# Attention outputs joined on ScalarE and GpSimd instead of VectorE, and one swap in the order of the up product

## The chip, the cores and the metric

The kernel runs on one core of a Trainium2 chip. The metric is the device time of one execution in microseconds (us). A core has five engines that each work through a list of instructions in order: TensorE (PE; its weight loads are shown apart, as PEld), VectorE (DVE), ScalarE (ACT), GpSimd (POOL) and SyncE (SP), which here only issues DMAs. Engines wait for each other by semaphores. Matmul results land in PSUM, in banks of 512 float32 columns on 128 partitions; everything else is in SBUF.

## The reference

One transformer block on 1024 tokens of width 1024, all in float32. Two mixers run on the same normalised input: softmax attention with a forget gate (8 heads of 64), and an RWKV-7 recurrence. Their outputs are gated, merged and projected; a feed-forward part with a short convolution and a gate follows.

```python
u = modulate(rms_norm(h, ln1_g), shift1, scale1)
proj = u @ w_in                                   # q, k, v, f | rwkv | gates
logits = q @ k.T * scale + cum[:, None] - cum[None, :]
o_fox = softmax(where(causal, logits, -inf)) @ v  # per head, 64 wide
merged = sigmoid(p_gate_fox) * (o_fox @ fox_w_out) + sigmoid(p_gate_rwkv) * (o_rwkv @ rwkv_w_out)
h = h + gate1 * (merged @ w_o)
u2 = modulate(rms_norm(h, ln2_g), shift2, scale2)
a, b = split(u2 @ w_up)                           # 2816 columns each
h = h + gate2 * ((silu(conv3(a) + conv_b) * b) @ w_down)
return rms_norm(h, final_g)
```

## The kernel before

Every float32 matrix is held as two parts of the fast matmul type, a high part (a rounded copy, made on ScalarE or GpSimd) and a low part (the rest, by a VectorE subtraction); a product is then three matmuls, high by high, high by low and low by high. Stages follow each other: the input projection, the RWKV recurrence, attention, the branch projections (br), w_o, the up product, and the down product.

**Attention.** Query rows are taken 256 at a time, so each head has four groups I, and a group goes through these steps:

- lg: the logits of two row blocks go to a PSUM bank pair. `softmax` takes the row maximum on VectorE (L1049, into nm), the exponential with its sum on ScalarE (L1053, into P), the reciprocal and the scaling of P on VectorE (L1058, L1059).
- tp: TensorE transposes P. `halve` copies the high part to th on ScalarE (L1086) and makes the low part tl on VectorE (L1089).
- ov: TensorE multiplies the values vh, whose 128 columns hold the high and the low part of 64 value columns, by th and tl. The result fills one bank of 128 rows by 256 columns: 64 rows of the high part's product and 64 of the low part's. There is one such bank, ov_ps.
- `collect` adds the two halves of the bank's rows: ScalarE copies one half to o (L1120), VectorE adds the other half from PSUM (L1122). When both heads of a pair have filled o, GpSimd splits it into fx (L1129, L1130); in the last head ScalarE and VectorE do that.

Between these steps TensorE computes the gate products (rk_ps, one bank) that were left over from before. ScalarE and VectorE evacuate them (`gate_out`, L1162 to L1170). GpSimd also casts their weights (hi_in, L266) and issues the loads of the next heads (stA L995, stB L997, vh L999), each of which waits until the tile it overwrites has been read.

The order of all this on TensorE, VectorE and ScalarE is written by a planner, class Weave, while the program is built. It holds a clock for TensorE, by the cost of each matmul, and clocks for ScalarE and VectorE, which `weave.use` moves by a cost; every chain yields the time until its next step is due, and gate products fill TensorE's time in between. `ov_free` holds the planned time at which the bank is free. GpSimd's and SyncE's instructions in this stage are placed by the framework's scheduler.

After attention, `br_load` loads a branch weight (raw_br, L1210) and `br_open` casts it, the first on GpSimd (L1223), the others on ScalarE (L1221), and loads a gate (L1226). The first br products are br0 and br1 of the first token half.

**Up product.** It is computed as a seven-product scheme per pair of column tiles: (i, k) is product k for tile i, with one operand made from w_up (A or S, high part on ScalarE L1481, low part on VectorE L1485) and one made from the activations (B11, T3, T2, T4, T1, B22; `T_split`, ScalarE L1722, VectorE L1724). Product 4 uses T4, product 5 uses T1, product 3 uses B22. Products 1, 6, 5 and 3 of one i add up in one bank, X; 7 and 4 in another, Y. Between them `up_evac` reads the sum so far: L1559 copies, L1564 adds Y into U after product 4, L1566 adds X into Z after product 5 (for i = 0 and 1 that tile is called Ze). The table `plan` sets the order of products; `up_to` makes the operands a few products ahead, and here SP, VectorE, ScalarE, GpSimd and TensorE all run in the order of the code. For i = 0 and 1 the T matrices themselves are still being made between the first products.

Of the kernel before, what the change touches and what calls it, by code (L numbers as in the profile page):

```python
# [9 lines left out]
F32 = mybir.dt.float32  # L10
F32R = mybir.dt.float32r
AF = mybir.ActivationFunctionType
ALU = mybir.AluOpType
# [119 lines left out]
def hybrid_block(ctx: ExitStack, tc: tile.TileContext, a, out):  # L133
    nc = tc.nc
    weave = Weave()
# [30 lines left out]
    def V(name, i=0, n=1):  # L166
        o, _ = VEC[name]
        return vec[:, o + i : o + i + n]
# [12 lines left out]

    omu = cp.tile([128, 14], F32, name="omu")
    nc.vector.tensor_scalar(omu, V("mu", 0, 14), -1.0, 1.0, op0=ALU.mult, op1=ALU.add)
    nw0 = cp.tile([128, 4], F32, name="nw0")
    nc.vector.tensor_scalar(nw0, V("w0", 0, 4), -1.0, None, op0=ALU.mult)
    na0 = cp.tile([128, 4], F32, name="na0")
    nc.vector.tensor_scalar(na0, V("a0", 0, 4), -1.0, None, op0=ALU.mult)
    nkk = cp.tile([128, 4], F32, name="nkk")
    nc.vector.tensor_scalar(nkk, V("k_k", 0, 4), -1.0, None, op0=ALU.mult)
    oka = cp.tile([128, 4], F32, name="oka")  # L190
    nc.vector.tensor_scalar(oka, V("k_a", 0, 4), -1.0, 1.0, op0=ALU.mult, op1=ALU.add)
    sc = cp.tile([128, 8], F32, name="sc")
    sig_c = nc.scalar.activation(sc, V("c", 0, 8), AF.Sigmoid)
# [794 lines left out]
    at = es.enter_context(tc.tile_pool(name="at", bufs=2, reuse_waits="tile"))  # L988
# [21 lines left out]
    with tc.manual_schedule(engines={mybir.EngineType.DVE, mybir.EngineType.Activation}):  # L1010
        seq = [(h, I) for h in range(8) for I in ((0, 1, 3, 2) if h == 7 else (3, 0, 2, 1))]
        lg_free, tp_free, pl_free, ps_free, th_free, ov_free = (deque([0.0] * n) for n in (2, 2, 4, 2, 3, 1))
        probs, av_queue, halves = {}, deque(), {}
        ov_ps = pb.tile([128, NH], F32, tag="big", name="ov")[:, 0:256]
        rk_ps = pb.tile([128, NH], F32, tag="big", name="rk_ps")

# [28 lines left out]
                    yield 0  # L1045

        def softmax(h, i, n, lg):
            nm = at.tile([128, 3], F32, tag="nm", name=f"nm{h}_{i}", bufs=4)
            nc.vector.tensor_reduce(nm[:, 0:1], lg[:, 0:n], axis=AX.X, op=ALU.max, negate=True)  # L1049
            yield weave.use("DVE", weave.now, 70 + 1.04 * n) + 140 - weave.now  # L1050
            e = (at.tile([128, S], F32, tag="P", name=f"P{h}_{i}", bufs=4) if i > 3 else
                 at.tile([128, NH], F32, tag="Ps", name=f"P{h}_{i}", bufs=2))
            nc.scalar.activation(e[:, 0:n], lg[:, 0:n], AF.Exp, bias=nm[:, 0:1], accum_out=nm[:, 1:2])  # L1053
            t = weave.use("ACT", weave.now, 250 + 0.83 * n)
            if i > 3 or i % 2:
                lg_free.append(t + 210)
            yield t + 140 - weave.now
            nc.vector.reciprocal(nm[:, 2:3], nm[:, 1:2])  # L1058
            ts(e[:, 0:n], e[:, 0:n], nm[:, 2:3], None, op0=ALU.mult)  # L1059
            t = weave.use("DVE", weave.now, 230 + 0.53 * n)  # L1060
            probs[h, i] = t + 210, e
# [32 lines left out]
        def a_chain():  # L1094

            for _ in range(8 * 10):
                while not av_queue:
                    yield 100
                t, h, I, jj, th, tl = av_queue.popleft()
                yield t - weave.now  # L1100
                if jj == 0:
                    yield from slot(ov_free)
                vh = heads[h][2]
                order = [(0, th), (1, th), (1, tl), (0, tl)] if jj == I else [(0, th), (0, tl), (1, th), (1, tl)]
                for x, (k, t) in enumerate(order):
                    o0 = 128 if (jj == I and k == 1) else 0
                    mm(ov_ps[:, o0:256], vh[:, 2 * jj + k, :], t[:, 256 * k : 256 * k + 256 - o0],
                       start=jj == 0 and x == 0, stop=jj == I and x == 3)
                th_free.append(weave.now + 260)
                if jj == I:  # L1110
                    weave.spawn(collect(h, I), 260)
                yield 0

        def collect(h, I):
            p, hf, oc = h // 2, I // 2, slice(I % 2 * 256, I % 2 * 256 + 256)
            rows = slice(h % 2 * 64, h % 2 * 64 + 64)
            if (p, hf) not in halves:
                halves[p, hf] = at.tile([128, NH], F32, tag="o", name=f"o{p}{hf}"), []
            o, got = halves[p, hf]
            nc.scalar.copy(o[rows, oc], ov_ps[rows, :])  # L1120
            yield weave.use("ACT", weave.now, 270) + 140 - weave.now
            tt(o[rows, oc], o[rows, oc], ov_ps[64 - h % 2 * 64 : 128 - h % 2 * 64, :], op=ALU.add)  # L1122
            t = weave.use("DVE", weave.now, 340) + 140
            ov_free.append(t + 70)
            got.append(I)
            if len(got) == 4:
                cs = slice(hf * NH, hf * NH + NH)
                if h < 7:
                    nc.gpsimd.tensor_copy(fx[0][p][:, cs], o)  # L1129
                    nc.gpsimd.tensor_tensor(fx[1][p][:, cs], o, f32(fx[0][p][:, cs]), op=ALU.subtract)  # L1130
                    return
                yield t - weave.now
                nc.scalar.copy(fx[0][p][:, cs], o)
                yield weave.use("ACT", weave.now, 530) + 140 - weave.now
                tt(fx[1][p][:, cs], o, f32(fx[0][p][:, cs]), op=ALU.subtract)
# [95 lines left out]
    if "rest" in marks:  # L1231
        g, m = (gsp.tile([128, NH], F32, tag="sp0", name=f"rest{k}") for k in range(2))
        i = nc.scalar.activation(g, marks["rest"], AF.Abs)
# [89 lines left out]
    for x in range(2):  # L1323
        for n in range(8):
            if x or n:
                k = 8 * x + n + 1
# [277 lines left out]
        put(6, s1[:, NH:])  # L1604

    plan = [(i, k) for ks in ((1, 2), (7,), (6,)) for i in range(2) for k in ks]
    plan += [(0, 4), (0, 5), (1, 5), (1, 4), (0, 3), (1, 3)] + [(2, k) for k in (1, 7, 6, 2, 4, 5)]
    for i in range(3, NFF):
        plan += [(i, 1), (i, 7), (i - 1, 3)] + [(i, k) for k in ((6, 2, 4, 5) if i < NFF - 1 else (6, 2, 5, 4))]
    plan.append((NFF - 1, 3))  # L1610
# [116 lines left out]
    for n in range(4):  # L1727
# [4 lines left out]
        if n in (1, 2):  # L1732
            kts = (0, 1) if n == 1 else (2, 3)
            turn2(1, [kt + 4 * j for kt in kts for j in range(2)], (2, 3, 4, 5), [U[j][kt] for kt in kts for j in range(2)],
                  rows=((0, 1, 2), (3,)) if n == 1 else ((0, 1, 2, 3),), by_dve=(1, 3) if n == 2 else ())
# [302 lines left out]
```

## Time and profile before

| what | value |
| --- | --- |
| median of three timed runs | 1654.52 us |
| the three runs | 1647.03, 1654.52, 1655.5 us |
| profiled execution, its own time | 1648.91 us |
| its span, first to last instruction | 1647.1 us |
| granted TensorE clock | 0.995 of full speed |
| attention outputs (first to last ov product) | 640 to 820 us |
| T4 and T1 made, first products with them | 1025 to 1043 us |

The profile is one execution. Its views name instructions by line, engine, operation and tiles (out<-in). A row of a timeline gives start, length, the instruction, and in brackets the idle time of the engine before it and what ended it. A row of waits gives who waited, for whom, total us, how often, and the longest. A row of groups gives busy us, the mean of one in ns, and the idle time before.

### The profile page before, as it was taken

The page shows a single profiled execution, that of the slowest core. Times are in us where ns is not written, and L with a number is a line of the kernel's source. Part 1 is how long each engine was busy: PE and PEld are TensorE (multiplying, and loading weights), DVE is VectorE, ACT ScalarE, POOL GpSimd, SP SyncE. Part 2 cuts the span into 40 slices and gives each one's busy share as a digit, 9 for nine tenths or more (in the row PEclk, how much of TensorE's full clock was granted, in tenths as well). Part 3 has the DMA queues.
Part 4 walks back from the last instruction along what each step waited for, and adds up shares of the span by engine and source line. Part 5 has one row for each costly group of instructions (what it writes and reads, how often), then busy time and mean ns, then how long its engine had stood idle before and what let it go on. Part 6 is the DMA issues. An engine that isn't in the chain of part 4 may idle for free.

```text
span 1647.1 us, 25947 instructions
## 1 busy us (share of the span) xinstructions
PE 1607.8 (98%) x9694; PEld 1339.6 (81%) x9694; DVE 1222.6 (74%) x2373; ACT 820.9 (50%) x1537; POOL 130.8 (8%) x153
## 2 busy tenths in 40 slices
PE   7999999999999999999999999999999999999998
PEld 7777788798978788888888888788888888888886
DVE  5786787878876526888679447887777777886677
ACT  5563335445445646766623235644444444555455
POOL 0011101111111010221022000000000000000000
PEclk9999999999999999999999999999999999999999
DMA  8488645543332346433197420242232232675363
GB/s 339 138 326 242 178 123 143 134 123 94 107 115 85 97 126 157 129 117 106 56 353 270 168 81 26 84 134 97 96 119 98 96 109 96 225 254 160 122 211 109
DMA packets 121645, 240.59 MB, mean 146 GB/s; under 512 B 40048, under 2 KB 48880, under 8 KB 121520
## 3 DMA queue, kind: packets, MB, share of 16 engines
q1 hardware_dynamic: 113040, 220.58, 41.0%
q0 software_dynamic: 8480, 18.37, 4.2%
q8 instruction: 76, 1.25, 0.3%
q14 instruction: 49, 0.40, 0.1%
HBM read 173.35 MB, written 65.54 MB: 145 GB/s over the span
## 4 chain that ended last, share of the span: by engine, by line
PE 58%; DVE 5%; ACT 2%; DMA 2%; issue 1%; SPq 0%; ACTq 0%; DVEq 0%
PE X L141 13%; PE D L141 13%; PE Y L141 6%; PE wo L141 5%; PE br L141 4%; PE rk_ps L141 3%; PE W L141 3%; PE gt L141 3%; PE lg L141 2%; PE ov L141 2%; PE tp L145 2%; DMA d_gate<-gs 1%; DVE nm L1049 1%; DVE P L1059 1%; DVE tl L1089 0%
## 5 line engine op out<-in xcount | busy, mean ns | idle before, releaser
L141 PE MATMUL D<-op,op 128*128 128x512 f32 x924 | 209.8, 389 | 0.0
L141 PEld LDWEIGHTS D<-op,op 128*128 128x128 f32 x924 | 173.3, 188 | 36.3 <-DVE op L1261 0.3
L141 PE MATMUL X<-T_m,S 128*128 128x512 f32 x440 | 107.8, 390 | 1.6 <-ACT T_m L1722 1.1
L141 PEld LDWEIGHTS X<-T_m,S 128*128 128x128 f32 x440 | 82.4, 188 | 20.4 <-ACT T_m L1722 2.5
L1260 ACT CAST op<-g 128x512 fp32r<-128x512 f32 x77 | 47.8, 621 | 73.8 <-PE D L141 49.0
L1261 DVE TENSOR_TENSOR op<-g,op 128x512 fp32r<-128x512 f32 x77 | 53.0, 688 | 41.4 <-ACT op L1260 41.4
L1519 DVE SCALAR_TENSOR_TENSOR c<-ab,vec,c 128x512 f32<-128x512 f32 x88 | 65.9, 750 | 18.4 <-ACT c L1522 16.8
L784 DVE TENSOR_TENSOR t<-E,M 128x60 f32<-128x60 f32 (+24 forms) x248 | 55.6, 224 | 27.9 <-DMA M<-sm 21.8
L1485 DVE TENSOR_TENSOR A<-ur,A 128x512 fp32r<-128x512 f32 x64 | 44.0, 688 | 38.7 <-ACT A L1481 38.5
L1485 DVE TENSOR_TENSOR S<-ur,S 128x512 fp32r<-128x512 f32 x66 | 45.5, 691 | 35.2 <-ACT S L1481 35.1
L274 DVE TENSOR_TENSOR lo_in<-raw_in,hi_in 128x512 fp32r<-128x512 f32 x84 | 56.7, 712 | 17.6 <-PE gt L141 4.8
L1481 ACT CAST S<-ur 128x512 fp32r<-128x512 f32 x66 | 41.0, 622 | 55.8 <-DVE ur L1474 30.6
L141 PE MATMUL Y<-T_h,S 128*128 128x512 f32 x264 | 63.6, 390 | 0.4 <-ACT T_h L1740 0.4
L141 PE MATMUL Y<-T_h,A 128*128 128x512 f32 x264 | 63.7, 389 | 0.3 <-ACT T_h L1722 0.3
L1053 ACT ACTIVATE P<-lg,nm 128x896 f32<-128x896 f32 (+3 forms) x64 | 47.4, 743 | 30.7 <-DVE nm L1049 22.5
L1481 ACT CAST A<-ur 128x512 fp32r<-128x512 f32 x64 | 39.6, 622 | 43.1 <-PE X L141 31.3
L786 DVE TENSOR_TENSOR E<-E,t 128x60 f32<-128x60 f32 (+24 forms) x248 | 56.2, 227 | 6.4
L141 PE MATMUL W<-B_f,A 128*128 128x512 f32 x252 | 60.6, 389 | 0.0
L141 PE MATMUL X<-B_b,A 128*128 128x512 f32 x252 | 60.5, 389 | 0.0
L141 PEld LDWEIGHTS Y<-T_h,S 128*128 128x128 f32 x264 | 49.5, 188 | 11.1 <-ACT T_h L1740 0.8
L141 PEld LDWEIGHTS Y<-T_h,A 128*128 128x128 f32 x264 | 49.5, 188 | 10.9 <-ACT T_h L1722 0.7
L272 ACT CAST hi_in<-raw_in 128x1024 fp32r<-128x1024 f32 x42 | 43.8, 1048 | 26.3 <-PE ps_rkv L141 11.3
(483 smaller groups left out, 4134.4 us busy)
## 6 DMA issues: line engine op xcount, KB each, us to landing
raw_in<-in_w_in SPq DMA_DIRECT2D x50, 512.0 KB, 4.0
wm<-in_w_mod SPq DMA_DIRECT2D x48, 512.0 KB, 7.3
ur<-in_w_up SPq DMA_DIRECT2D x44, 512.0 KB, 3.8
g<-d_g SPq DMA_DIRECT2D x35, 512.0 KB, 4.0
d_g<-gs SPq DMA_DIRECT2D x44, 256.0 KB, 2.0
d_g<-c SPq DMA_DIRECT2D x33, 256.0 KB, 4.4
d_st<-qh SPq DMA_DIRECT2D x64, 128.0 KB, 2.5
stA<-d_st POOLq DMA_DIRECT2D x8, 1024.0 KB, 6.9
```

The costliest lines, as they stand in the source:

```text
L141: nc.tensor.matmul(o, lhsT, rhs, start=start, stop=stop, skip_group_check=more)
L145: nc.tensor.transpose(o, i, eye)
L272: nc.scalar.copy(hi, raw)
L274: nc.vector.tensor_tensor(lo[:, c : c + NH], raw[:, c : c + NH], f32(hi[:, c : c + NH]), op=ALU.subtract)
L784: tt(tv, E32[:, 0:J, s : s + 1].to_broadcast([128, J, W]), M32[:, s : s + 1, s + 1 : 32].to_broadcast([128, J, W]), op=ALU.mult)
L786: tt(E32[:, 0:J, s + 1 : 32], E32[:, 0:J, s + 1 : 32], tv, op=ALU.add)
L1053: nc.scalar.activation(e[:, 0:n], lg[:, 0:n], AF.Exp, bias=nm[:, 0:1], accum_out=nm[:, 1:2])
L1260: nc.scalar.copy(hi, src)
L1261: tt(lo, src, f32(hi), op=ALU.subtract)
L1481: nc.scalar.copy(hi, src)
L1485: tt(lo, src, f32(hi), op=ALU.subtract)
L1519: stt(c, ab[:, x + hf * NH : x + hf * NH + NH], V("conv_w", 22 * x + i), c, op0=ALU.mult, op1=ALU.add)
```

## The change

In `collect`, for heads 0 to 6, ScalarE copies both halves of the bank's rows, the second into a new tile o2 (one buffer), the bank counts as free after that, and GpSimd adds o2 to o in SBUF. Head 7 keeps VectorE's add. The planner charges ScalarE 560 ns for both copies, and VectorE nothing. To make room, four small constants share one tile, and the four rotating nm tiles become columns of one. In the up product's table, (1, 4) moves ahead of (0, 5) and (1, 5).

```diff
-    nw0 = cp.tile([128, 4], F32, name="nw0")
+    quads = cp.tile([128, 16], F32, name="quads")
+    nw0, na0, nkk, oka = (quads[:, 4 * x : 4 * x + 4] for x in range(4))
...
+        nm_all = at.tile([128, 12], F32, tag="nm", name="nm", bufs=1)
+        nms = deque(nm_all[:, 3 * x : 3 * x + 3] for x in range(4))
...
-            nm = at.tile([128, 3], F32, tag="nm", name=f"nm{h}_{i}", bufs=4)
+            nms.append(nms.popleft())
+            nm = nms[0]
...
             nc.scalar.copy(o[rows, oc], ov_ps[rows, :])
-            yield weave.use("ACT", weave.now, 270) + 140 - weave.now
-            tt(o[rows, oc], o[rows, oc], ov_ps[64 - h % 2 * 64 : 128 - h % 2 * 64, :], op=ALU.add)
-            t = weave.use("DVE", weave.now, 340) + 140
-            ov_free.append(t + 70)
+            others = ov_ps[64 - h % 2 * 64 : 128 - h % 2 * 64, :]
+            if h < 7:
+                o2 = at.tile([128, 256], F32, tag="o2", name=f"o2_{h}_{I}", bufs=1)
+                nc.scalar.copy(o2[rows, :], others)
+                yield weave.use("ACT", weave.now, 560) + 140 - weave.now
+                ov_free.append(weave.now + 70)
+                nc.gpsimd.tensor_tensor(o[rows, oc], o[rows, oc], o2[rows, :], op=ALU.add)
+            else:
+                yield weave.use("ACT", weave.now, 270) + 140 - weave.now
+                tt(o[rows, oc], o[rows, oc], others, op=ALU.add)
+                t = weave.use("DVE", weave.now, 340) + 140
+                ov_free.append(t + 70)
...
-    plan += [(0, 4), (0, 5), (1, 5), (1, 4), (0, 3), (1, 3)] + [(2, k) for k in (1, 7, 6, 2, 4, 5)]
+    plan += [(0, 4), (1, 4), (0, 5), (1, 5), (0, 3), (1, 3)] + [(2, k) for k in (1, 7, 6, 2, 4, 5)]
```

GpSimd's list in the first two heads of attention, before (line numbers of the kernel before):

```order
97 L995 DMA stA_7209<-d_st 128x2x1024
98 L997 DMA stB_7211<-d_st 68x2x1024
99 L266 CAST hi_in_7318<-raw_in_7316 128x1024
100 L999 DMA vh_7213<-d_v 128x1024
101 L995 DMA stA_7490<-d_st 128x2x1024
102 L997 DMA stB_7492<-d_st 68x2x1024
```

The same place now (line numbers of the changed kernel; o2 of head 1, group 3 is o_1_3):

```order
97 L993 DMA stA_7212<-d_st 128x2x1024
98 L995 DMA stB_7214<-d_st 68x2x1024
99 L1128 TENSOR_TENSOR o_7135<-o_7135,o_0_3_7137 64x256
100 L1128 TENSOR_TENSOR o_7186<-o_7186,o_0_0_7188 64x256
101 L264 CAST hi_in_7323<-raw_in_7321 128x1024
102 L1128 TENSOR_TENSOR o_7135<-o_7135,o_0_2_7255 64x256
103 L997 DMA vh_7216<-d_v 128x1024
104 L1128 TENSOR_TENSOR o_7186<-o_7186,o_0_1_7319 64x256
105 L1128 TENSOR_TENSOR o_7135<-o_7135,o_1_3_7426 64x256
106 L993 DMA stA_7525<-d_st 128x2x1024
107 L995 DMA stB_7527<-d_st 68x2x1024
```

The adds stand among the weight cast and the DMA issues, in the order in which the groups are collected.

TensorE at the end of attention, before: from the last transposes (tp of head 7, group 2) to the first br product.

```order
2232 L145 MATMUL tp_22_9186<-cst,P_5_9087 128x128 x2
2233 L141 MATMUL ov<-th_21_9171,vh_8622 128x256
2234 L141 MATMUL ov<-tl_21_9179,vh_8622 128x256
2235 L141 MATMUL ov<-th_21_9171,vh_8622 128x256
2236 L141 MATMUL ov<-tl_21_9179,vh_8622 128x256
2237 L141 MATMUL rk_ps<-u_hi,lo_in_8681 128x512 x7
2238 L141 MATMUL ov<-th_22_9194,vh_8622 128x256
2239 L141 MATMUL ov<-th_22_9194,vh_8622 128x128
2240 L141 MATMUL ov<-tl_22_9199,vh_8622 128x128
2241 L141 MATMUL ov<-tl_22_9199,vh_8622 128x256
2242 L141 MATMUL rk_ps<-u_hi,lo_in_8681 128x512
2243 L141 MATMUL br_00_9288<-fx_6842,hi_br_9232 128x512
```

The same place now, without the last rows of ov and the br product, which follow as before:

```order
2225 L141 MATMUL rk_ps<-u_hi,lo_in_8560 128x512 x2
2226 L145 MATMUL tp_22_9178<-cst,P_4_9053 128x128
2227 L145 MATMUL tp_22_9178<-cst,P_5_9108 128x128 x2
2228 L141 MATMUL ov<-th_20_9163,vh_8608 128x256
2229 L141 MATMUL ov<-tl_20_9172,vh_8608 128x256
2230 L141 MATMUL ov<-th_20_9163,vh_8608 128x256
2231 L141 MATMUL ov<-tl_20_9172,vh_8608 128x256
2232 L141 MATMUL ov<-th_21_9175,vh_8608 128x256
2233 L141 MATMUL ov<-tl_21_9182,vh_8608 128x256
2234 L141 MATMUL ov<-th_21_9175,vh_8608 128x256
2235 L141 MATMUL ov<-tl_21_9182,vh_8608 128x256
2236 L141 MATMUL ov<-th_22_9188,vh_8608 128x256
```

Eight gate products (seven and one) that stood behind the last transposes now stand ahead of them, and four ov products that stood ahead now stand behind.

VectorE in the up product, before, from T1's last low parts on (T_e is T1's low part, B_m is B22's; the first S and A are operands of products 5 and 4, ur and the S behind it make S4 of product 3):

```order
1493 L1724 TENSOR_TENSOR T_e_10909<-uf_e_10386,T_m_10907 128x512 x2
1494 L1485 TENSOR_TENSOR S_1_10918<-ur_10422,S_1_10918 128x512
1495 L1564 TENSOR_TENSOR U_10886<-Y_10824,U_10886 128x512
1496 L1724 TENSOR_TENSOR B_m_10936<-u_m_10665,B_e_10934 128x512 x2
1497 L1724 TENSOR_TENSOR B_m_10937<-u_m_10666,B_e_10935 128x512 x2
1498 L1485 TENSOR_TENSOR A_1_10946<-ur_10422,A_1_10946 128x512
1499 L1566 TENSOR_TENSOR Ze_a_10662<-X_10678,Ze_a_10662 128x512
1500 L1477 TENSOR_TENSOR ur_10309<-ur_10309 128x512
1501 L1485 TENSOR_TENSOR S_0_10963<-ur_10309,S_0_10963 128x512
1502 L1566 TENSOR_TENSOR Ze_a_10662<-X_10750,Ze_a_10662 128x512
1503 L1477 TENSOR_TENSOR ur_10421<-ur_10421 128x512
1504 L1485 TENSOR_TENSOR S_1_10984<-ur_10421,S_1_10984 128x512
```

The same place now:

```order
1457 L1733 TENSOR_TENSOR T_e_10899<-uf_e_10376,T_m_10897 128x512 x2
1458 L1494 TENSOR_TENSOR S_0_10908<-ur_10300,S_0_10908 128x512
1459 L1573 TENSOR_TENSOR U_10876<-Y_10814,U_10876 128x512
1460 L1733 TENSOR_TENSOR B_m_10926<-u_m_10655,B_e_10924 128x512 x2
1461 L1733 TENSOR_TENSOR B_m_10927<-u_m_10656,B_e_10925 128x512 x2
1462 L1494 TENSOR_TENSOR S_1_10936<-ur_10412,S_1_10936 128x512
1463 L1573 TENSOR_TENSOR U_10890<-Y_10831,U_10890 128x512
1464 L1486 TENSOR_TENSOR ur_10299<-ur_10299 128x512
1465 L1494 TENSOR_TENSOR S_0_10953<-ur_10299,S_0_10953 128x512
1466 L1575 TENSOR_TENSOR Ze_a_10652<-X_10668,Ze_a_10652 128x512
1467 L1486 TENSOR_TENSOR ur_10411<-ur_10411 128x512
1468 L1494 TENSOR_TENSOR S_1_10974<-ur_10411,S_1_10974 128x512
```

The operands of product 4 for i = 1 have moved ahead of those of product 5, and the reads of X into Ze, which free the bank for product 3, have moved two places back for i = 0; the one for i = 1 follows two rows after the last shown.

More of the change, by code (lines that the diff above doesn't have):

```diff
@@ L183, in hybrid_block @@
     nc.vector.tensor_scalar(omu, V("mu", 0, 14), -1.0, 1.0, op0=ALU.mult, op1=ALU.add)
-    nw0 = cp.tile([128, 4], F32, name="nw0")
+    quads = cp.tile([128, 16], F32, name="quads")
+    nw0, na0, nkk, oka = (quads[:, 4 * x : 4 * x + 4] for x in range(4))
     nc.vector.tensor_scalar(nw0, V("w0", 0, 4), -1.0, None, op0=ALU.mult)
-    na0 = cp.tile([128, 4], F32, name="na0")
     nc.vector.tensor_scalar(na0, V("a0", 0, 4), -1.0, None, op0=ALU.mult)
-    nkk = cp.tile([128, 4], F32, name="nkk")
     nc.vector.tensor_scalar(nkk, V("k_k", 0, 4), -1.0, None, op0=ALU.mult)
-    oka = cp.tile([128, 4], F32, name="oka")
     nc.vector.tensor_scalar(oka, V("k_a", 0, 4), -1.0, 1.0, op0=ALU.mult, op1=ALU.add)
```

## The prediction

> **What bounds the kernel now.** I read the page's engine row first.
>
> ```profile
> PE 1607.8 (98%) x9694; PEld 1339.6 (81%) x9694; DVE 1222.6 (74%) x2373; ACT 820.9 (50%) x1537; POOL 130.8 (8%) x153
> ```
>
> TensorE is busy nearly all the time, so an edit on another engine can only win time where TensorE waits. The first edit acts in the attention stage. I took the timeline of the attention outputs (the ov products, from 640 to 820 us) and asked for the busy time of the engines there.
>
> ```profile
> core 0: us, PE busy (x) PEld busy (x) DVE busy (x) ACT busy (x) POOL busy (x), PEclk, DMA share, GB/s
> 640.00:820.00 180.00, 173.30 (x1097) 151.72 (x1097) 151.57 (x308) 122.76 (x283) 31.10 (x36) 1.00 0.35 100
> ```
>
> The columns after the length are TensorE, its weight loads, VectorE, ScalarE and GpSimd: of 180 us TensorE has 6.7 without a matmul, VectorE 28 without work, ScalarE 57, GpSimd 149. A matmul is shown with its full 0.39 us though the next can start after 0.23, so the waits of the weight loads, which run ahead of the products, tell better how late an operand was. They are the next view, for the same stretch:
>
> ```profile
> PEld ov L141 <- DVE o L1122: 3.3, 4, 2.4
> PEld ov L141 <- DVE tl L1089: 3.1, 5, 1.1
> PEld lg L141 <- ACT P L1053: 2.7, 4, 1.2
> PEld rk_ps L141 <- issue: 1.1, 1, 1.1
> PEld ov L141 <- ACT th L1086: 0.7, 1, 0.7
> PEld tp L145 <- DVE P L1059: 0.6, 2, 0.3
> ...
> PEld tp L145 <- PE tp L145: 0.3, 1, 0.3
> ```
>
> (Six and the last of twelve rows, which sum to 13.6 us; the columns are the total, the times and the longest.) So 13.6 us is all that any edit in this stretch could win, and VectorE ends 7 us of it. The largest single wait shows how:
>
> ```profile
> 672.10 0.37 ACT L1120 COPY o<-ov 64x256 f32<-64x256 f32 x1 [0.58 <-PE ov L141]
> ...
> 675.41 0.42 DVE L1122 TENSOR_TENSOR o<-o,ov 64x256 f32<-64x256 f32 x1
> ...
> 675.88 0.39 PE L141 MATMUL ov<-th,vh 128*128 128x256 f32 x1 [1.98 <-DVE o L1122]
> ```
>
> ScalarE's copy had ended at 672.5, but the add that frees the one ov bank stood in VectorE's queue until 675.4, and TensorE stood still for it.
>
> **Part one: the attention outputs.** Costs of the operations, from the groups of instructions from 640 to 824 us, which hold all 32 outputs:
>
> ```profile
> L1122 DVE TENSOR_TENSOR o<-o,ov 64x256 f32<-64x256 f32 x32 | 13.4, 420 | 7.2 <-ACT o L1120 6.3
> L1120 ACT COPY o<-ov 64x256 f32<-64x256 f32 x32 | 11.7, 366 | 11.7 <-PE ov L141 11.2 <-issue 0.2
> ...
> L1130 POOL TENSOR_TENSOR fx<-o,fx 128x512 fp32r<-128x512 f32 x6 | 7.9, 1310 | 0.4
> ...
> L997 POOL DMA_DIRECT2D stB<-d_st x6 | 6.0, 994 | 0.0
> ...
> L995 POOL DMA_DIRECT2D stA<-d_st x6 | 4.3, 714 | 49.0 <-PE lg L141 48.8
> ```
>
> *VectorE* loses 28 of the 32 adds: 28 x 0.42 = 11.8 us of 151.7. *ScalarE* gains 28 copies of the shape of L1120: 28 x 0.366 = 10.3 us, on 122.8 of 180, so it keeps 47 us idle. *GpSimd* gains 28 adds of 64x256, which the trace does not show there. Bounds: not below the same add on VectorE, 0.42 us, and not above its own add of twice the columns, 1.31 us; I take half of that, 0.65, since it is the same operation on the same engine. That is 18 us on an engine with 149 idle; at 1.31 it would be 37, still covered.
>
> The bank is now free when the second copy ends, directly behind the first, and no place in VectorE's queue lies between. The 3.3 us of the first row go. What is late next is tl (3.1 us) and the scaling of P (0.6), both on VectorE, whose idle time grows from 28 to about 40 us of 180; I count half of them, 1.9 us. ScalarE's two rows (2.7 and 0.7) I leave: it waits less for VectorE, but carries the copies. Gain: 3.3 + 1.9 = 5.2 us, bounded by 0 and 13.6.
>
> The edit adds a wait: with one o2 buffer, ScalarE's second copy waits for GpSimd's previous add, and behind that copy stand the casts th and the exponentials. GpSimd's adds stand behind its DMA issues and its cast of hi_in. The 32 outputs of 180 us follow each other by 5.6 us on average, and what can stand ahead of an add is one issue of stA and stB (0.71 + 0.99 us) with the wait for its buffer, which ends with products of about the same time: zero in the forecast. If the adds came one whole distance late each time, ScalarE would stand still and the case would be the second rival's.
>
> The re-planned order of TensorE costs something at the end. In head 7 the last gate products (rk_ps) are used up earlier, so eight of them no longer stand between the last transposes and the first br product groups:
>
> ```profile
> 818.12 1.76 PE L141 MATMUL rk_ps<-u_hi,lo_in 128*128 128x512 f32 x7
> 819.72 0.34 PE L141 MATMUL ov<-th,vh 128*128 128x256 f32 x2
> 819.90 0.44 PE L141 MATMUL ov<-tl,vh 128*128 128x128 f32 x2
> 820.18 0.40 PE L141 MATMUL rk_ps<-u_hi,lo_in 128*128 128x512 f32 x1
> 820.41 2.02 PE L141 MATMUL br<-fx,hi_br 128*128 128x512 f32 x8
> ...
> 823.21 2.11 PE L141 MATMUL br<-fx,hi_br 128*128 128x512 f32 x8
> ```
>
> ```profile
> 818.02 0.38 SPq L1210 DMA_DIRECT2D raw_br<-in_w_br  x1
> ```
>
> ```profile
> 822.53 0.62 ACT L1221 CAST hi_br<-raw_br 128x512 fp32r<-128x512 f32 x1 [0.69 <-DMA raw_br<-in_w_br]
> ```
>
> The load of raw_br is issued after those transposes, at 818.0, and the second br group starts when its cast ends, at 823.2; TensorE arrived there just in time. In the new order it has eight gate products less in that stretch (7 from 818.12 to 819.72, so 8 are 1.83 us) and four ov products more (0.46, as from 819.72 to 820.18), so it arrives 1.4 us early and waits. Cost: 1.4 us, between 0 (if it arrives late anyway) and 1.8.
>
> **Part two: T4 ahead of T1.** Products (0,4) and (1,4) now run first, then (0,5), (1,5), (0,3). The rows of before:
>
> ```profile
> 1030.13 2.33 PE L141 MATMUL Y<-T_h,A 128*128 128x512 f32 x9 [0.28 <-ACT T_h L1722]
> 1033.36 1.02 PE L141 MATMUL X<-T_m,S 128*128 128x512 f32 x2 [0.90 <-ACT T_m L1722]
> ...
> 1039.98 2.88 PE L141 MATMUL Y<-T_h,A 128*128 128x512 f32 x12
> 1042.70 1.98 PE L141 MATMUL X<-B_e,S 128*128 128x512 f32 x8
> ...
> 1054.26 3.04 PE L141 MATMUL X<-T_m,S 128*128 128x512 f32 x12 [0.52 <-ACT x L1559]
> ```
>
> ```profile
> 1034.94 0.62 ACT L1481 CAST S<-ur 128x512 fp32r<-128x512 f32 x1
> ```
>
> ```profile
> 1036.13 0.68 DVE L1485 TENSOR_TENSOR S<-ur,S 128x512 fp32r<-128x512 f32 x1
> ...
> 1039.74 0.68 DVE L1485 TENSOR_TENSOR A<-ur,A 128x512 fp32r<-128x512 f32 x1
> ...
> 1042.92 0.68 DVE L1566 TENSOR_TENSOR Ze_a<-X,Ze_a 128x512 f32<-128x512 f32 x1
> ...
> 1046.10 0.68 DVE L1564 TENSOR_TENSOR U<-Y,U 128x512 f32<-128x512 f32 x1
> ```
>
> A product of 12 matmuls takes 2.72 us (1039.98 to 1042.70). Product (1,4) fills the 0.9 us wait for T1's first cast: it runs from 1032.2 (1030.13 and nine times 0.227) to 1034.9. Product (0,5) then needs S of i=0, whose cast now stands where S of i=1 stood, ending at 1035.6, and whose low part ends at 1036.8: it runs from 1035.6 to 1038.7. Product (1,5) needs a low part that stands where A's stood, ending at 1040.4: it ends at 1042.3, against 1042.70 for the three products before. So far 0.4 us are won. But product (0,3) adds into the bank that L1566 reads, and that read has moved behind the low part of S4, to the place of the row at 1042.92, ending at 1043.6; (0,3) runs from 1043.6 to 1046.4. The read for i=1 has moved to the place of the row at 1046.10, ending at 1046.8; (1,3) ends at 1049.5, where it ended at 1042.70 + 2 x 2.72 = 1048.1. That is 1.4 us late. The wait at 1054.26 for a ScalarE copy, 0.52 us shown and 0.7 between starts, takes up half. Cost: 0.7 us, between 0 (if the low parts come sooner) and 1.4.
>
> **Sum.** -5.2 + 1.4 + 0.7 = -3.1 us. The freed constants (one tile for four, one nm tile) only move addresses: nothing. The profiled execution took 1648.9 us, the three timed runs 1647.0, 1654.5 and 1655.5: one kernel, four readings 8 us apart. The mean of the middle two is 1651.7, and I set the sum against it: **1648.6 us**; against the profiled execution itself it is 1645.8. About 0.5%, 8.3 us, is what a measurement of this kernel can tell from no change.
>
> **Rivals.**
>
> *Every wait goes.* VectorE was the only late engine, and ScalarE's lateness came from waiting on it. For: ScalarE's exponentials stand idle for VectorE's maxima, in the waits from 615 to 824 us:
>
> ```profile
> ACT P L1053 <- DVE nm L1049: 22.5, 18, 5.8
> ```
>
> Against: ScalarE's extra 10.3 us. Time: -13.6 + 2.1 = -11.5, 1640.2 us. Chance 0.20.
>
> *The waits return elsewhere.* The new order puts each ov group as tightly as the plan allows, and 5.2 us of new waits, on ScalarE or on tl, replace the old: +2.1, 1653.8 us. For: the plan kept TensorE full in both orders. Against: one bank-release chain is shorter for certain. Chance 0.18.
>
> *GpSimd's adds hold up VectorE.* The trace has this already:
>
> ```profile
> 725.77 1.81 DVE L1059 TENSOR_SCALAR P<-P,nm 128x256 f32<-128x256 f32 x1
> ```
>
> ```profile
> 726.13 1.29 POOL L1130 TENSOR_TENSOR fx<-o,fx 128x512 fp32r<-128x512 f32 x1
> ```
>
> ```profile
> L1059 DVE TENSOR_SCALAR P<-P,nm 128x384 f32<-128x384 f32 x8 | 3.4, 420 | 0.3
> ```
>
> A scaling of 256 columns took 1.81 us, where 384 columns take 0.42: it ended when GpSimd's add did. If each of the 28 new adds stops a VectorE operation for its whole length, VectorE pays 28 x 0.65 = 18.2 us for the 11.8 it is spared, 6.4 us more than now, all of it on operations that TensorE waits for: +6.4 + 2.1 = +8.5, 1660.2 us. It decides as soon as more than two in three of the adds (11.8 of 18.2) meet such an operation. Against: the eight scalings of 384 columns average an undisturbed 0.42 us though GpSimd worked 31 us of this stretch, and VectorE's maxima and tl read a bank. Chance 0.17. [...]
>
> **How the numbers follow.** Forecast 0.45, the three rivals 0.20, 0.18 and 0.17. Faster by over 0.5%: the first rival and a twentieth from the forecast's lower edge, 0.25. Slower: the last, 0.17. Same: 0.58. The range goes from the first rival to the last, 1640 to 1660 us, which also holds the 8 us between readings; forecast and second rival lie inside it.
>
> **What would show it.** Right: no wait on L1122 in heads 0 to 6, VectorE near 140 us in the ov stretch with GpSimd near 49, a wait of 1 to 2 us at the second br group behind a raw_br load, and X of (0,3) waiting for the Ze add. Wrong: weight loads waiting for ScalarE's second copy or for th by more than 3 us; scalings of P over twice their usual length in most heads; GpSimd's add over 1 us; TensorE idle in the stretch unchanged or larger.

## The result, and the profile after

| kernel | median | runs | ratio to before, 95% interval |
| --- | --- | --- | --- |
| before | 1648.72 us | 9 (1645.97 to 1655.5) | |
| changed | 1658.44 us | 9 (1656.95 to 1663.71) | 1.0057 (1.0042 to 1.0072) |

The change makes the kernel 9.7 us slower. The forecast was 3.1 us faster: 1648.6 us, from a base taken as 1651.7. The profiled execution took 1659.27 us with a span of 1657.5, at a granted clock of 0.996 (before 0.995).

The engine row of the page, the window of the attention outputs, and the new operations there (groups of instructions from 640 to 824 us):

```profile
PE 1615.9 (97%) x9694; PEld 1338.9 (81%) x9694; DVE 1215.7 (73%) x2345; ACT 833.0 (50%) x1565; POOL 153.9 (9%) x181
```

```profile
640.00:820.00 180.00, 173.73 (x1095) 151.98 (x1094) 143.72 (x282) 135.73 (x314) 50.90 (x63) 1.00 0.34 98
```

```profile
L1128 POOL TENSOR_TENSOR o<-o,o 64x256 f32<-64x256 f32 x28 | 20.9, 747 | 72.9 <-ACT o L1125 72.5
...
L1125 ACT COPY o<-ov 64x256 f32<-64x256 f32 x28 | 10.3, 368 | 0.7
```

The attention edit did what it says: VectorE has 8 us less work there, ScalarE 13 more, GpSimd 20 more. But TensorE as a whole is busy 8.1 us *longer* (1607.8 to 1615.9) with the same 9694 matmuls, and the window of the attention outputs holds only 0.4 us of it (173.30 to 173.73). So I compared where each stage begins, by the first product of each in TensorE's timeline of the two traces:

| stretch | before | changed |
| --- | --- | --- |
| up to the first ov | 639.7 us | 641.1 |
| ov to br | 180.7 | 180.3 |
| br to w_o | 88.1 | 89.6 |
| w_o to up product | 94.4 | 96.3 |
| up product to down product | 426.9 | 432.0 |
| down product, first to last | 209.8 | 210.7 |

(The first stretch varies by up to 9 us between executions, as the last section shows.) Half of the loss is in the up product, and it grows there steadily, with no wait. TensorE's timeline of one round of that product, before:

```profile
1195.86 1.98 PE L141 MATMUL X<-T_m,S 128*128 128x512 f32 x8
1197.67 1.07 PE L141 MATMUL X<-T_e,S 128*128 128x512 f32 x4
1198.58 2.88 PE L141 MATMUL X<-B_b,A 128*128 128x512 f32 x12
1201.30 2.88 PE L141 MATMUL Y<-T_h,S 128*128 128x512 f32 x12
...
1206.74 2.88 PE L141 MATMUL X<-T_m,S 128*128 128x512 f32 x12
1209.46 2.88 PE L141 MATMUL W<-B_f,A 128*128 128x512 f32 x12
1212.18 2.88 PE L141 MATMUL Y<-T_h,A 128*128 128x512 f32 x12
1214.90 1.98 PE L141 MATMUL X<-T_m,S 128*128 128x512 f32 x8
```

and after:

```profile
1202.65 2.01 PE L141 MATMUL X<-T_m,S 128*128 128x512 f32 x8
1204.50 1.08 PE L141 MATMUL X<-T_e,S 128*128 128x512 f32 x4
1205.41 2.93 PE L141 MATMUL X<-B_b,A 128*128 128x512 f32 x12
1208.18 2.88 PE L141 MATMUL Y<-T_h,S 128*128 128x512 f32 x12
...
1213.67 2.91 PE L141 MATMUL X<-T_m,S 128*128 128x512 f32 x12
1216.41 2.93 PE L141 MATMUL W<-B_f,A 128*128 128x512 f32 x12
1219.18 2.88 PE L141 MATMUL Y<-T_h,A 128*128 128x512 f32 x12
1221.90 2.01 PE L141 MATMUL X<-T_m,S 128*128 128x512 f32 x8
```

One round is 84 matmuls, from one X<-T_m,S x8 to the next: 19.04 us before (226.7 ns each), 19.25 after (229.2). No row has an idle time in brackets. The products with T_h run as before (12 in 2.72 us); T_m, T_e, B_b and B_f are slower, and in the same way in every round. A wait for another engine would hardly repeat so exactly, so I looked for something fixed in the program. The change that reaches the up product in a fixed way is the one that the prediction priced at nothing: four constants in one tile.

In the built programs the four tiles of 16 bytes stand 32 bytes apart, so they took 128 bytes of a partition, and the one tile of 64 bytes takes 64. All pools stacked above them (T_h, B_f, B_b, S, A, the operands of br and w_o) moved down by 64 bytes. T_m, T_e, B_e, B_m and u lie in pools that are stacked down from the top of SBUF, and did not move.

### The profile page after: what moved, and what is told of

Read it like the earlier page. It is cut to its first block, busy times and chain, and to the rows that moved or that the text cites. A ratio compares the mean times of both kernels' runs of the same rounds, so it can differ in the third digit from the quotient of the medians.

```text
span 1657.5 us, 25953 instructions
## 1 busy us (share of the span) xinstructions
PE 1615.9 (97%) x9694; PEld 1338.9 (81%) x9694; DVE 1215.7 (73%) x2345; ACT 833.0 (50%) x1565; POOL 153.9 (9%) x181
## 4 chain that ended last, share of the span: by engine, by line
PE 68%; DVE 8%; ACT 3%; DMA 2%; issue 1%; SPq 1%; DVEq 0%; ACTq 0%
PE X L141 14%; PE D L141 13%; PE Y L141 7%; PE wo L141 5%; PE gt L141 5%; PE br L141 4%; PE rk_ps L141 4%; PE W L141 3%; PE ps_rkv L141 3%; PE ov L141 2%; PE lg L141 2%; PE tp L145 1%; PE v L141 1%; DVE t L782 1%; DMA M<-sm 1%
## 5 line engine op out<-in xcount | busy, mean ns | idle before, releaser
L141 PE MATMUL D<-op,op 128*128 128x512 f32 x924 | 210.7, 390 | 0.0
L1090 DVE TENSOR_TENSOR tl<-tp,th 128x512 fp32r<-128x512 f32 (+1 forms) x80 | 49.9, 631 | 15.1 <-ACT th L1087 14.6
L1050 DVE TENSOR_REDUCE nm<-lg 128x1 f32<-128x896 f32 (+3 forms) x64 | 46.8, 751 | 13.9 <-PE lg L141 7.6
```

Source lines behind the costliest of these rows:

```text
L141: nc.tensor.matmul(o, lhsT, rhs, start=start, stop=stop, skip_group_check=more)
L1090: tt(tl[:, 0:w], tp[:, 0:w], f32(th[:, 0:w]), op=ALU.subtract)
```

## The experiments

**Which of the edits it is.** Four kernels: the constants alone, the swap alone, all edits with the left-hand pools 128 bytes lower instead of 64, and the latter without the swap.

```diff
# small_tiles_alone, against before
-    nw0 = cp.tile([128, 4], F32, name="nw0")
...
+    quads = cp.tile([128, 16], F32, name="quads")
+    nw0, na0, nkk, oka = (quads[:, 4 * x : 4 * x + 4] for x in range(4))
```

> The kernel before with one edit: the four 128x4 constants in one tile of 128x16. Each tile takes a multiple of 32 bytes of a partition, so four tiles took 128 bytes and one takes 64: all tiles of the pools stacked above move down by 64 bytes, those of the right-hand pools (T_m, T_e, B_e, B_m, u) stay. No instruction is added, removed or reordered. Theory P (places: a matmul is slower where the addresses of its two operands differ by an odd multiple of 64 bytes): X<-T_m,S at a pitch of about 230 ns instead of 226.7, the time +6 to +10 us. Rival E (the two edits in attention and in the up product cost the 9.7 us themselves): no change, within 2 us of the kernel before.

Measured: 1658.49 us, ratio 1.0064 (1.0047 to 1.0081). One round of the up product lasts 19.25 us, from these two rows:

```profile
1207.39 2.01 PE L141 MATMUL X<-T_m,S 128*128 128x512 f32 x8
...
1226.64 2.01 PE L141 MATMUL X<-T_m,S 128*128 128x512 f32 x8
```

An edit that adds, removes and reorders no instruction of the up product costs as much as the whole change. Rival E, which put the loss down to the two edits in attention and the up product, falls.

```diff
# swap_alone, against before
-    plan += [(0, 4), (0, 5), (1, 5), (1, 4), (0, 3), (1, 3)] + ...
+    plan += [(0, 4), (1, 4), (0, 5), (1, 5), (0, 3), (1, 3)] + ...
```

> The kernel before with the order of the up product changed alone ((1,4) ahead of (0,5) and (1,5)). Theory P: +0.7 us (between 0 and +1.4, the prediction's own term), up-product pitch 226.7 ns throughout. Rival E: a part of the 9.7 us, +3 us or more, with waits behind the Ze adds and U adds that the prediction did not see.

Measured: 1651.03 us, ratio 1.0011 (0.9998 to 1.0023). In the trace the stretch from the first up product to the first down product is 427.66 us (1004.75 to 1432.41), 0.77 longer than before. The rows are the predicted ones:

```profile
1037.47 2.46 PE L141 MATMUL X<-T_m,S 128*128 128x512 f32 x8 [0.43 <-ACT S L1481]
...
1042.34 1.19 PE L141 MATMUL X<-T_m,S 128*128 128x512 f32 x4 [0.58 <-DVE S L1485]
...
1045.62 2.09 PE L141 MATMUL X<-B_e,S 128*128 128x512 f32 x8 [1.17 <-DVE Ze_a L1566]
```

Product (0,3), X<-B_e,S, stands still for VectorE's read of its bank.

```diff
# both_edits_128, against the changed kernel
-    quads = cp.tile([128, 16], F32, name="quads")
-    nw0, na0, nkk, oka = (quads[:, 4 * x : 4 * x + 4] for x in range(4))
+    nw0, na0, nkk, oka = (top[:, 4 * x : 4 * x + 4] for x in range(4))
-        nm_all = at.tile([128, 12], F32, tag="nm", name="nm", bufs=1)
+        nm_all = at.tile([128, 32], F32, tag="nm", name="nm", bufs=1)
```

> The changed kernel with all its edits, but the four constants lie in the unused 96-byte tile at the top of SBUF and nm's tile has 32 columns: all tiles of the left-hand pools then stand 128 bytes lower than in the kernel before, not 64 (addresses equal modulo 128). Instructions and their order as in the changed kernel. Theory P: the pitch of the up product is back at 226.7 ns and the time at that of the kernel before, -1 to +1 us. Rival E: as the changed kernel, about +9.7 us.

> The same without the swap in the up product: only the attention outputs are joined on ScalarE and GpSimd, with all tiles 128 bytes lower. Theory P: -0.4 to -1.5 us against the kernel before (what the stretch of the attention outputs gained in the trace after, less the start of the branch products), so 0.7 us under the same kernel with the swap. The prediction's term for this edit was -3.8 (-5.2 and +1.4). Rival E: +6 us or more.

Measured: 1658.18 us, 1.0063 (1.0048 to 1.0079), and 1657.68 us, 1.0058 (1.0039 to 1.0077). My expectation was wrong: 128 bytes lower is no better than 64.

```profile
1204.06 2.02 PE L141 MATMUL X<-T_m,S 128*128 128x512 f32 x8
...
1223.35 2.02 PE L141 MATMUL X<-T_m,S 128*128 128x512 f32 x8
```

A round of both_edits_128 lasts 19.29 us. "Equal modulo 128" falls; that places matter does not, since the products with T_m became slower still. I took the tile addresses of all kernels and the starts of all 128x512 matmuls from five traces (before, changed, small_tiles_alone, swap_alone, both_edits_128), and grouped the mean pitch (from the start of one matmul to the start of the next) in the up and down products by moving address less stationary address, modulo 256: 0: 227.4 ns (11274 matmuls), 64: 229.9 (1588), 128: 232.9 (841), 192: 233.4 (68). In the kernel before all these pairs agree modulo 256, but for 12 matmuls. That is theory P2 of the next runs. (The moving operand is the one of 512 columns, the first name behind the arrow; the stationary one is that of the weight load, the second.)

**The edits at the old addresses.** With nm in a tile at the top of SBUF that nothing used, the four constants can keep their four tiles, and o2 still fits.

```diff
# both_edits_home, against the changed kernel (joined_outputs_home: also the old plan)
-    quads = cp.tile([128, 16], F32, name="quads")
...
+    nw0 = cp.tile([128, 4], F32, name="nw0")
...
-        nm_all = at.tile([128, 12], F32, tag="nm", name="nm", bufs=1)
-        nms = deque(nm_all[:, 3 * x : 3 * x + 3] for x in range(4))
+        nms = deque(top[:, 3 * x : 3 * x + 3] for x in range(4))
```

> All edits of the changed kernel, but the four constants stay in four tiles and nm lies in the unused tile at the top of SBUF. Every tile but P, th, tl and o of attention then has the address that it has in the kernel before; instructions and order are those of the changed kernel. Theory P2 (a matmul is slow where the addresses of its two operands differ modulo 256 bytes; 64 costs some 3 ns of 227, 128 some 6.5): pitch of X<-T_m,S back at 226.7 ns, the time +1.4 us against the kernel before (the swap's +1.8 as measured alone, less 0.4 in attention; between 0 and +3). Rival E (edits and addresses hurt each by itself, together not more): +6 us or more.

> The same without the swap in the up product: the attention edit alone, nothing else moved. Theory P2: -0.4 us against the kernel before (between -1.5 and +0.5), since the waits of the weight loads from 640 to 820 us were 13.6 us before and 13.1 in the trace after. The prediction's own term would be -3.8. Rival E: +4 us or more.

Measured: 1648.2 us, 0.9989 (0.9976 to 1.0002), and 1647.54 us, 0.9983 (0.9972 to 0.9994). The same instructions in the same order as in the changed kernel, at other addresses, take 10 us less. The round is 19.04 us again:

```profile
1213.03 1.98 PE L141 MATMUL X<-T_m,S 128*128 128x512 f32 x8
...
1232.07 1.98 PE L141 MATMUL X<-T_m,S 128*128 128x512 f32 x8
```

joined_outputs_home, the attention edit without the swap, is the version that beats the kernel before, by 2.8 us (1.0 to 4.6). Both kernels came out faster than expected (+1.4, between 0 and +3, and -0.4, between -1.5 and +0.5), and not all of that is the edit's. In the trace of joined_outputs_home the ov to br stretch is only 0.17 us shorter than in the trace before (180.54 for 180.71), and br to w_o is 0.86 shorter (87.23 for 88.09). The latter belongs to the place of nm: it lasts 87.2 us in all five kernels with nm in the tile at the top, nm_at_top among them, whose attention is that of before. The experiments on attention below say what else there is.

**Difference or address.** Three kernels move the two sides against each other and together.

```diff
# small_tiles_both_sides: before with quads (left 64 lower), and right 64 lower
-    ....tile([128, 24], F32, name="top")
+    ....tile([128, 40], F32, name="top")
# right_64_up: before with only this
+    ....tile([128, 8], F32, name="top")
# left_64_up: before with only this
+    cp.tile([128, 16], F32, name="filler")
```

> The kernel before with the constants in one tile (left-hand pools 64 bytes lower) and the unused tile at the top 64 bytes larger (right-hand pools 64 bytes lower too). No operand has its old address, but nearly all pairs have their old difference modulo 256. Theory P2 (the difference decides): pitch 226.7 ns, the time within 1 us of the kernel before, against +9.2 with the left side moved alone. Rival A (the address itself decides: tiles must start at 128 modulo 256): +9 us or more, B_f and T_m both at 230 ns.

> The kernel before with the unused tile at the top of SBUF 64 bytes smaller: the right-hand pools (T_m, T_e, B_e, B_m, u, the low operands of w_o) stand 64 bytes higher, all constants and left-hand tiles stay. Moving less stationary is 64 modulo 256 for X<-T_m,S, as in the changed kernel, but by moving the other operand. Theory P2: X<-T_m,S at 229.7 ns, W<-B_f,A at 230.8, the time +9 us. Rival A (tiles on the left must stand at 128 modulo 256): no change for products with both operands on the left, +4 us at most.

> The kernel before with an unused 64-byte tile among the constants: the left-hand pools stand 64 bytes higher, nothing else is edited. Moving less stationary address is then 192 modulo 256 for X<-T_m,S where the changed kernel has 64. Theory P2 (the difference modulo 256 decides, and not its sign alone): the few products with 192 in the runs so far had a pitch of 233.4 ns, so X<-T_m,S at 233 ns (229.7 in the changed kernel) and the time +8 to +12 us. Rival S (what counts is only the smaller distance, 64 both ways): 229.7 ns and +9 us.

| kernel | left, right (modulo 256) | round | median | ratio |
| --- | --- | --- | --- | --- |
| before | 128, 128 | 19.04 us | 1648.72 us | |
| small_tiles_both_sides | 64, 64 | 19.04 | 1650.59 | 1.0003 (0.999 to 1.0016) |
| small_tiles_alone | 64, 128 | 19.25 | 1658.49 | 1.0064 (1.0047 to 1.0081) |
| right_64_up | 128, 192 | 19.26 | 1658.34 | 1.0049 (1.0031 to 1.0067) |
| both_edits_128 | 0, 128 | 19.29 | 1658.18 | 1.0063 (1.0048 to 1.0079) |
| left_64_up | 192, 128 | 19.32 | 1658.0 | 1.0046 (1.0029 to 1.0063) |

(Each ratio is to the runs of before that were made beside it, with medians of 1649.25 to 1649.62 us.) Moving both sides alike costs nothing measurable, with no operand of the up product at its old place; moving either side alone costs 8 to 9 us. The difference decides, so rival A falls. The pitch of X<-T_m,S (mean distance of the starts, those under 300 ns) was 229.7 ns in right_64_up and 233.3 in left_64_up, as P2 had it, and rival S falls for this product. The expected larger total for left_64_up did not come (+7.6 us by its ratio, 4.8 to 10.4): the products with B_f and B_b were less slow there (228.5 ns for 231.0), and w_o to up product lost 1.0 us (95.4 for 94.4) where in right_64_up it lost 1.9.

One row speaks against P2 as it stands, though its number was expected. In right_64_up, B_f and A have not moved and agree modulo 256, yet W<-B_f,A is slow:

```profile
1213.16 2.91 PE L141 MATMUL X<-T_m,S 128*128 128x512 f32 x12
1215.91 2.93 PE L141 MATMUL W<-B_f,A 128*128 128x512 f32 x12
1218.68 2.88 PE L141 MATMUL Y<-T_h,A 128*128 128x512 f32 x12
```

Its 12 starts are 235, 230, 234, 236, 224, 231, 235, 229, 232, 231, 227 and 226 ns apart, and the next product, Y, is clean. A mismatch in one product (X<-T_m,S) thus seems to reach some ten matmuls into the next. Why the difference of two addresses costs time, and why it reaches on, was not found out.

**Where the attention gain went.** Two kernels at the old addresses, without the swap: one adds on VectorE in SBUF, and one leaves the second half of the rows of heads 0 to 6 out.

```diff
# joined_on_vector, against joined_outputs_home
-                nc.gpsimd.tensor_tensor(o[rows, oc], o[rows, oc], o2[rows, :], op=ALU.add)
+                tt(o[rows, oc], o[rows, oc], o2[rows, :], op=ALU.add)
+                weave.use("DVE", weave.now, 340)
# no_second_half: neither o2, nor its copy, nor the add
```

> The attention edit alone at the old addresses, but the add of o2 in SBUF is done on VectorE instead of GpSimd (ScalarE still copies both halves, the bank is free after its second copy). It asks what the move to GpSimd was worth. In the trace after, VectorE's scalings of P took 37.8 us in sum where they took 33.6, and lo_in 7.5 for 6.4, while GpSimd's 28 adds took 20.9. If GpSimd's adds hold VectorE up and that is what ate the gain: faster than with GpSimd, -1 us or more. If VectorE's own work ate it: slower than with GpSimd, by up to 2 us. If ScalarE's second copies did: the same within 1 us.

> The attention edit at the old addresses, but for heads 0 to 6 the second half of the bank's rows is left out: ScalarE copies one half, the bank is free, no second copy and no add anywhere. It bounds what any way of joining the halves can win. If the bank's release was worth what the prediction counted (5.2 us) and ScalarE's second copies ate it: -5 us or more against the kernel before, ov waiting for tl under 3 us. If the waits in this stretch only change their name: -1 to -3 us, no more than with the joining.

> The kernel before with only nm moved into the unused tile at the top, so that P, th, tl and o of attention stand 128 bytes lower (th then agrees with vh modulo 256, where before it differed by 128); no other edit. It asks whether the -2.8 us of the attention edit at the old addresses came from this move. If the ov products (256 columns) pay for a difference as the 512-column ones do: 128 x 2 products by some 1 to 6 ns, -0.3 to -1.5 us. If the joining of the outputs made all of the gain: no change, within 1 us.

Measured: joined_on_vector 1648.47 us, 0.9993 (0.9982 to 1.0004); no_second_half 1646.17 us, 0.9977 (0.9964 to 0.999); nm_at_top, which is the kernel before with nm moved as in these, 1648.17 us, 0.9991 (0.9977 to 1.0005). The ov to br stretch, by the first products of the two, lasted 180.5 us in joined_outputs_home, 181.2 in joined_on_vector and 178.5 in no_second_half. So GpSimd is worth 0.7 us against VectorE, from one trace of each, and against the 180.7 of the kernel before the most that a joining behind ScalarE's first copy could win there is 2.2 us. The time of no_second_half, -3.8 us by its ratio (-5.9 to -1.6), lies between what its two cases had; 0.9 of it is again the place of nm.

But in nm_at_top, whose attention is that of before, the stretch lasted 182.3. So moving nm gained nothing there; its -1.5 us by the ratio (-3.8 to +0.8) is not clear of zero, and of the -2.8 above it leaves open how much is the joining's. I compared the stretch over all traces whose attention is unchanged: 180.7 and 180.8 us (before, small_tiles_both_sides), and 182.2 to 182.4 in the other five. The windows show the reason, here swap_alone (182.2 us) and then before, over the same 10 us:

```profile
675.00:680.00 5.00, 3.66 (x21) 3.57 (x22) 4.80 (x10) 4.70 (x10) 0.00 (x0) 0.77 0.41 103
680.00:685.00 5.00, 5.00 (x34) 4.67 (x33) 3.64 (x11) 3.15 (x10) 2.23 (x3) 0.88 0.28 90
```

```profile
675.00:680.00 5.00, 4.12 (x32) 3.93 (x32) 4.77 (x11) 4.74 (x10) 0.08 (x1) 1.00 0.37 95
680.00:685.00 5.00, 5.00 (x36) 4.59 (x35) 4.80 (x13) 3.72 (x10) 2.91 (x4) 1.00 0.46 128
```

The wait of 1.98 us for L1122, which the prediction quoted, stands here (1.93 to 1.99 us in the seven), and in five of seven executions the granted clock falls behind it, to between 0.69 and 0.80 in the lowest window of 5 us. In the profiled execution of before it happens not to. In the five traces in which ScalarE and GpSimd join the halves, and in joined_on_vector and no_second_half, that long wait is gone and the clock is 1.00 from 640 to 820 us; the stretch lasts 180.3 to 180.6 in the five. The edit thus gains 0.1 to 0.5 us against an execution without the dip and 1.6 to 2.0 against one with it, 1.3 on the mean (181.8 less 180.5). That the wait brings the dip is read from these 14 traces; no run tests it by itself.

The waits of the weight loads say what ate the rest of the gain. The changed kernel, 640 to 826 us (six of seven rows):

```profile
PEld ov L141 <- DVE tl L1090: 5.7, 9, 1.5
PEld lg L141 <- ACT P L1054: 2.0, 7, 0.6
PEld ov L141 <- ACT o L1125: 2.0, 3, 0.8
PEld br L141 <- ACT hi_br L1230: 1.4, 1, 1.4
PEld tp L145 <- DVE tl L1090: 1.4, 2, 0.9
PEld rk_ps L141 <- ACT gm L1172: 1.2, 2, 0.7
```

and no_second_half:

```profile
PEld ov L141 <- DVE tl L1091: 3.2, 5, 1.5
PEld ov L141 <- ACT o L1122: 1.4, 2, 0.9
PEld tp L145 <- DVE tl L1091: 1.2, 2, 0.8
```

The bank's wait shrank from 3.3 to 2.0 us (now for ScalarE's second copy), and the waits for tl grew from 3.4 (3.1 and 0.3) to 7.1; without the second copies they are 4.4. VectorE makes tl from th. Its groups show longer idle time for th (the last figures are the idle time before tl and what ended it; before, after, and no_second_half):

```profile
L1089 DVE TENSOR_TENSOR tl<-tp,th 128x512 fp32r<-128x512 f32 x47 | 31.6, 685 | 3.7 <-ACT th L1086 3.3
L1089 DVE TENSOR_TENSOR tl<-tp,th 128x384 fp32r<-128x384 f32 x32 | 17.6, 553 | 4.6 <-ACT th L1086 4.2
```

```profile
L1090 DVE TENSOR_TENSOR tl<-tp,th 128x512 fp32r<-128x512 f32 x48 | 32.7, 683 | 5.9 <-ACT th L1087 5.6
L1090 DVE TENSOR_TENSOR tl<-tp,th 128x384 fp32r<-128x384 f32 x32 | 17.6, 552 | 9.2 <-ACT th L1087 9.0
```

```profile
L1091 DVE TENSOR_TENSOR tl<-tp,th 128x512 fp32r<-128x512 f32 x48 | 32.8, 685 | 4.4 <-ACT th L1088 4.3
L1091 DVE TENSOR_TENSOR tl<-tp,th 128x384 fp32r<-128x384 f32 x32 | 17.6, 553 | 9.4 <-ACT th L1088 9.4
```

This idle time went from 7.5 to 14.6 us, but it does not say that the second copies delay th: without them it is 13.7, and with them but with the adds on VectorE (joined_on_vector) it is 6.6. A VectorE with less work waits more. What does say it is the time from the end of the last transpose of a group to the start of its cast th, on the mean of the 80 casts: 0.60 us before, 0.74 in the changed kernel, 0.63 in no_second_half. The 10.3 us of second copies stand in ScalarE's queue among those casts, and without them th starts nearly as early as before.

## Why the prediction was wrong, step by step

- **"The freed constants only move addresses: nothing."** This is the step that failed: +9.2 us by itself (small_tiles_alone, the difference of the medians), of which 8.4 can be placed in its trace after the attention outputs: br to w_o 0.4, w_o to up product 1.9, up product 5.2, down product 0.9. The addresses relative to each other set the pitch of the matmuls (226.7 ns on the mean of a round of the up product before, 229.2 after), a term that the prediction put at nothing without asking. None of the rivals held it. That the other edits had nothing to do with it is shown by both_edits_home.
- **The attention gain, 5.2 us:** measured 0.1 to 2.0 in the ov to br stretch, 1.3 on the mean. The bank's release in VectorE's queue did go, but I priced ScalarE's copies by its idle total (57 us), not by what stands behind each copy. The prediction names the casts th there, and only considers a wait for o2. So the second rival's mechanism held inside attention: the waits from 640 to 820 us were 13.6 us and are 13.1 (the rows above without br, and 0.8 for issue), under other names. What is left of the gain is mostly the clock, as far as the traces above tell, a term that the prediction did not have.
- **GpSimd's add,** taken at 0.65 us: 0.747.
- **GpSimd holding VectorE:** it happens, at a fraction of the rival's price. The smallest scaling shows it, before and after:

```profile
L1059 DVE TENSOR_SCALAR P<-P,nm 128x128 f32<-128x128 f32 x7 | 2.0, 287 | 0.2
```

```profile
L1060 DVE TENSOR_SCALAR P<-P,nm 128x128 f32<-128x128 f32 x7 | 5.0, 717 | 0.2
```

  Two of these took 1.9 and 1.7 us, the others 0.29; the two ended 0.1 us after GpSimd's fx adds of 684.24 and 728.79 us (1.29 and 1.30 us long), an operation that the kernel before has too. Beside a new add (0.73 us) the scalings of 256 columns at 685.73 and 731.62 took 0.76 and 0.74 us, where four of the seven took 0.35. From joined_on_vector, which has no such adds on GpSimd, to joined_outputs_home the 64 scalings of attention went from 37.3 to 40.0 us and lo_in from 6.8 to 7.9: 3.8 us (4.9 against the kernel before) for 11.8 spared, under the point (all of it) from which that rival decides. VectorE's maxima and tl, which read a bank, kept their lengths beside the 20.9 us of new adds: tl of 512 columns took 685 ns before and 683 after (rows above), the maximum over 1024 columns 1217 and 1216. Why the scalings were held up and these were not is not shown. In the row at 725.77 us the scaling had begun 0.36 us before GpSimd's add at 726.13, and still took 1.81 us.
- **The tail, 1.4 us:** the br group waits 1.4 us for hi_br in the changed kernel (row above), as worked out. Against small_tiles_alone, with the same addresses in that stretch, br to w_o lasts 1.1 us longer (89.6 for 88.5). In joined_outputs_home the load came in time and no such row is left, so the term is between 0 and 1.4.
- **The swap, 0.7 us:** 0.77 in swap_alone, and 0.8 in both_edits_home (427.67 for 426.89), through the waits that were named.

The measured 1658.44 us lies near the 1660.2 of the rival in which GpSimd holds up VectorE, and inside the range. Both are luck: that rival's mechanism gave 4 to 5 us on VectorE, and without the constants the kernel is no slower than before.

Leaving out the constants, the prediction's sum was -3.1 us; both_edits_home measures -1.8 (-4.0 to +0.3). Its interval holds the sum, although the gain in attention was over-sized: the terms that were off are smaller than it can tell, and 0.9 us of the -1.8 is the place of nm.

## What to carry to other kernels

When an edit changes the size of any tile, list the addresses of the operands of the busiest matmuls before and after, as well as the order of instructions: here 64 bytes of constants decided, and the edits that the change was about did not. A loss that shows as busy time of TensorE with the same count of matmuls and no idle brackets is read from the starts of consecutive groups in the timeline, not from waits. And an engine's idle total does not price a new instruction on it; what stands behind that instruction in its queue does.

## What the runs showed of the hardware that I had not expected

- The pitch of a 128x512 float32r matmul depends on where its moving operand lies relative to its stationary one: 227.4 ns on the mean of the five traces above where the two addresses agree modulo 256 bytes (226.7 in a round of the kernel before), 229.9 where they differ by 64, 232.9 and 233.4 where they differ by 128 and 192; and in right_64_up a following product that agrees is slow for some ten matmuls (224 to 236 ns). Steps below 64 bytes were not tried. The pitch goes with the two addresses together; by what mechanism is not shown.
- A wait of TensorE of 1.93 to 1.99 us was followed by a lowered granted clock (0.69 to 0.80) in five of seven executions, and the stretch lasted some 1.5 us longer in those. Why the clock fell in five and not in the other two (before and small_tiles_both_sides, 1.00) is not shown.
- The start of the attention outputs varies between executions by up to 9 us (637.9 us in joined_outputs_home, 647.0 in nm_at_top). Much of the difference arises around 620 to 632 us, where TensorE waits for ScalarE's evacuation of a gate product (gm). The wait is 1.2 to 1.4 us in nine traces, at a clock of 1.00. It is 1.9 in the trace before, with a clock of 0.71 in the 4 us from 624. It is 4.7 to 5.4 in small_tiles_alone, joined_on_vector, nm_at_top and no_second_half, and there the clock falls to between 0.50 and 0.55. These four executions took 5 to 9 us more than the median of their kernels. Two rows of one of them:

```profile
624.00:628.00 4.00, 1.09 (x3) 0.90 (x4) 0.69 (x1) 3.21 (x6) 0.00 (x0) 0.77 1.25 205
628.00:632.00 4.00, 4.00 (x11) 3.13 (x10) 1.89 (x3) 0.67 (x2) 0.00 (x0) 0.50 0.83 167
```

  (joined_on_vector; the columns are those of the window rows above, the granted clock is 0.77 and then 0.50.) What makes ScalarE late there was not looked into. Stretches between two products therefore tell more than two spans do.
